# A decoder block on one core: other feed-forward groups, a mixer that ends earlier, and operands that are split where they land

## The chip, the cores and the metric

The kernel runs on one core of one Trainium2 chip. The metric is the device time of one execution in microseconds (us). TensorE (PE) multiplies matrices, VectorE (DVE) and ScalarE (ACT) do elementwise work, GpSimd (POOL) and SyncE (SP) issue the transfers. Every engine works through its instructions in order, and an instruction that waits holds up those behind it on the same engine.

## The reference

One layer of a decoder, 2048 positions of width 1024, all in fp32:

```python
mod = (silu(c) @ w_ada + b_ada)                       # shift, scale, gate, twice
h = rms_norm(x, norm1_g) * (1 + sc1) + sh1
gq, gk, gv, gr, glr, aq, ak, av = split(h @ w_in)
y_gla = gla_group(gq, gk, gv, log_sigmoid(glr @ w_gate + b) / 16, gr, gla_norm_g)   # 4 heads
y_att = dilated_attention_group(rms_norm(aq), rms_norm(ak), av)                     # 8 heads, 3 dilations
x = x + g1 * (concat(y_gla, y_att) @ w_out)
h = rms_norm(x, norm2_g) * (1 + sc2) + sh2
u_gate, u_val = split(causal_depthwise_conv(h @ w_up, conv_w, conv_b))              # width 3
x = x + g2 * ((silu(u_gate) * u_val) @ w_down)
```

w_up has 2 x 2816 columns, that is 22 pairs of 128-column blocks (a gate half and a value half); w_down has 2816 rows, 22 tiles of 128. The gated linear attention normalises its output per head by 1 / sqrt(mean square + eps).

## The kernel before

The sequence is cut into four chunks of 512 positions; everything is kept transposed, channels on the 128 partitions and positions along the row. An fp32 operand is split into a high part (rounded for the fast matmul) and a low part (the rest), and `mm3` (L308) makes each product of three matmuls: high by high, high by low, low by high. Weights are loaded as raw blocks of 512 KB on POOL's queue (L243), cast by ScalarE into whi (L248) and subtracted by VectorE into wlo (L249); `plan` (L258) lists the blocks in the order of their use and `weights` (L297) runs three blocks ahead, over two raw and four high and low slots.

The work is written as generators, and each `yield` ends a step. `beside(a, na, b, nb)` runs the steps of b and after each of them na/nb steps of a; what is left of a comes at the end. In `run` (L1159) the projections of all four chunks form `gemm` (27 of its steps are taken first). Then mixer 0 runs beside the rest of `gemm`, mixer 1 beside output projection 0 and feed-forward 0, mixer 2 beside output projection 1 and feed-forward 1, mixer 3 beside the next pair, and the last pair alone. The last steps of `gemm` are the channel blocks q6, g2, q7 and g3 of chunk 3's projection. A scheduler that simulates the program takes this order as its priorities and fixes the order of the instructions on each engine when the program is built; slots of a tile pool are waited for when none is free.

A mixer (`mix`, L1054) has two halves of gated linear attention (`gla`, L668) and four pairs of dilated attention heads (`attn`, L825). Each half ends with the per-head norm (L796 to L802): Ln and Exp on ScalarE make the inverse root. Each pair of heads ends with an addition into a stage tile (L1050) that is stored as block 4 + hp of y in DRAM (L1051).

`outproj` (L1062) loads the eight blocks of y (L1067) into tiles called sq, of which there are three, and splits each into hhi (ScalarE, L1076) and hlo (VectorE, L1077). For chunk 0 most of these parts lie in the slots ghi and glo (five each), which the q blocks of the projection use too; for the other chunks they lie in hhi and hlo (ten each), eight of which hold the feed-forward operand of the chunk before until its last up product. `soon` (L353) ties each load to a matmul some 20 contraction steps back. Eight blocks of 24 matmuls follow, evicted with the residual by VectorE (L1083), then the second norm's statistics, then the put-off product `self.tail`, and then the normalised and modulated operand (L476, L478, L480).

`ffn` (L1091) goes over groups of gate tiles: four, four, four, four, four and two. For each group it makes the up products (L1104, two blocks of 24 matmuls a tile), the conv (L1106 to L1113), the gate and its split into ghi and glo (L1117 to L1123), and then the down product of the group before (`down`, L1133): eight output blocks of three matmuls a gate tile, each added to the residual on VectorE (L1151). The last group's down product is not made there: it becomes `self.tail` and runs in the next chunk's output projection, after its eight blocks. Because the residual's tiles serve the next chunk by then, the next-to-last down product stores its eight blocks to DRAM (L1155), and the put-off one loads them again (L1148) into the slots y0 and y1 (two each), adds, and stores the result (L1153). Chunk 0's output projection has the last gate block of chunk 3's projection (`wide(1)`) as its tail. Four PSUM banks (psg) serve all of these products, four others (psa) the mixers.

Of the kernel before, what the change touches and what calls it, by code (L numbers as in the profile page):

```python
# [2 lines left out]

# [1 line left out]

# [5 lines left out]
F32 = mybir.dt.float32  # L11
# [8 lines left out]
P = 128  # L20
T = 512
NCH = 4
KD = 8
NF = 22
EPS = 1e-6
BIG = 1e30
GATE = 6
FIRST = (0, 1, 2, 3)
LEAD = 1

# [109 lines left out]
def chain(*gs):  # L140
    for g in gs:
        yield from g


class K:
# [112 lines left out]
    def plan(self):  # L258

        def proj(c):  # L260
            for o in ORDER if c else ORDER0:
                b = int(o[1])
                if c == NCH - 1 and o == "W1":
                    continue
                if o[0] == "W":
                    yield from (("w_tokw", (b, j), 2, T) for j in range(4))
                elif o[0] == "V":
                    yield from ((f"w_av{b}", (j,), 4, 256 if b else 272) for j in range(2))
                else:
                    b += 4 * (o[0] == "q")  # L270
                    if c or b not in FIRST:
                        yield "w_ch", (b,), KD, P

        def down(g):
            n = min(4, NF - 4 * g)
            yield from (("w_down", (4 * g + q,), n, 1024 // n) for q in range(n))

        def ffn(c):
            for g in range(6):
                for f in range(4 * g, min(4 * g + 4, NF)):  # L280
                    yield from (("w_up", (f + NF * half,), KD, P) for half in range(2))
                if g:
                    yield from down(g - 1)
            if c == NCH - 1:
                yield from down(5)

        for c in range(NCH):
            yield from proj(c)
        for c in range(NCH):
            yield from (("w_out", (b,), KD, P) for b in range(KD))  # L290
            if c:
                yield from down(5)
            else:
                yield from (("w_tokw", (1, j), 2, T) for j in range(4))
            yield from ffn(c)
# [372 lines left out]
    def gla(self, c, a):  # L668
# [106 lines left out]
        for s in range(2):  # L775
# [17 lines left out]
                nc.scalar.activation(jk[:, hd * P:(hd + 1) * P], o[:, hd * P:(hd + 1) * P], AF.Square, accum_out=ss[:, s, hd:hd + 1])  # L793
            os.append(o)
            yield
        nc.scalar.activation(ss, ss, AF.Ln, bias=self.eps, scale=1.0 / P)  # L796
        nc.scalar.activation(ss, ss, AF.Exp, scale=-0.5)
        ys = []
        for s in range(2):
            y = t2("pt", 5)  # L800
# [24 lines left out]
    def attn(self, c, hp, ready):  # L825
# [222 lines left out]
        st = self.at.tile([P, T], F32, name="stage", bufs=2)  # L1048
        nc.scalar.copy(st.rearrange("p (l j r) -> p r j l", j=4, r=4), O16.rearrange("p (r j l) -> p r j l", r=4, j=4))
        nc.vector.tensor_tensor(st.rearrange("p (l r) -> p r l", r=16), O.rearrange("p (r l) -> p r l", r=16), st.rearrange("p (l r) -> p r l", r=16), op=ALU.add)  # L1050
        nc.sync.dma_start(D[c]["y"][4 + hp], st)  # L1051
        yield

    def mix(self, c):  # L1054
# [7 lines left out]
    def outproj(self, c):  # L1062
        nc, A = self.nc, self.A
        hs = []
        for k in range(KD):
            t = self.tmp.tile([P, T], F32, name="sq", bufs=3)
            ld = self.dq.dma_start(t, self.D[c]["y"][k])  # L1067
            self.soon(ld)

            if c or k > 5:  # L1070
                hi, lo = (self.hp.tile([P, T], F32R, name=n) for n in ("hhi", "hlo"))
            elif k == 5:
                hi, lo = (self.up.tile([P, T], F32R, name=n, tag=n) for n in ("y0", "y1"))
            else:
                hi, lo = (self.gp.tile([P, T], F32R, name=n, tag=n) for n in ("ghi", "glo"))
            nc.scalar.copy(hi, t)  # L1076
            nc.vector.tensor_tensor(lo, t, hi.bitcast(F32), op=ALU.subtract)  # L1077
            hs.append((hi, lo))
        x1 = self.load_x(c)
        for cb in range(KD):  # L1080
            ps = self.pg()
            self.mm3(ps, self.weights("w_out", cb), hs)
            nc.vector.scalar_tensor_tensor(x1[cb], ps, self.mod[:, 16 + cb:17 + cb], x1[cb], op0=ALU.mult, op1=ALU.add)  # L1083
            yield
        self.x1[c] = x1
        rstd = self.norm_stats(lambda k: x1[k], not c)
        yield from self.tail
        self.h2[c] = self.norm_mod(lambda k: x1[k], rstd, self.G2, self.mod[:, 24:32], True)


    def ffn(self, c):  # L1091
        nc, A = self.nc, self.A
        x1, h2 = self.x1[c], self.h2[c]
        groups = [list(range(i, min(i + 4, NF))) for i in range(0, NF, 4)]
        pend = None
        for gi, grp in enumerate(groups + [None]):
            gs = []
            if grp is not None:
                for f in grp:
                    ys = []  # L1100
                    for half in range(2):
                        b = f + NF * half
                        ps = self.pg()
                        self.mm3(ps, self.weights("w_up", b), h2)  # L1104
                        y = self.up.tile([P, T], F32, name=f"y{half}")
                        nc.scalar.activation(y, ps, AF.Identity, bias=self.cb[:, b:b + 1], scale=self.cw[:, 2, b:b + 1])  # L1106
                        nc.vector.scalar_tensor_tensor(y[:, 1:], ps[:, :T - 1], self.cw[:, 1, b:b + 1], y[:, 1:], op0=ALU.mult, op1=ALU.add)  # L1107
                        nc.vector.scalar_tensor_tensor(y[:, 2:], ps[:, :T - 2], self.cw[:, 0, b:b + 1], y[:, 2:], op0=ALU.mult, op1=ALU.add)  # L1108
                        if c > 0:
                            nc.vector.scalar_tensor_tensor(y[:, :1], self.halo[:, b, 1:2], self.cw[:, 1, b:b + 1], y[:, :1], op0=ALU.mult, op1=ALU.add)  # L1110
                            nc.vector.scalar_tensor_tensor(y[:, :2], self.halo[:, b], self.cw[:, 0, b:b + 1], y[:, :2], op0=ALU.mult, op1=ALU.add)
                        if c < NCH - 1:
                            nc.scalar.copy(self.halo[:, b], ps[:, T - 2:])  # L1113
                        ys.append(y)
                        yield
                    th = self.up.tile([P, T], F32, name="th", bufs=1)
                    nc.scalar.activation(th, ys[0], AF.Tanh, scale=0.5)  # L1117
                    nc.vector.scalar_tensor_tensor(th, th, 1.0, ys[0], op0=ALU.add, op1=ALU.mult)
                    nc.vector.scalar_tensor_tensor(ys[1], th, 0.5, ys[1], op0=ALU.mult, op1=ALU.mult)
                    ghi = self.gp.tile([P, T], F32R, name="ghi", tag="ghi")  # L1120
                    nc.scalar.copy(ghi, ys[1])
                    glo = self.gp.tile([P, T], F32R, name="glo", tag="glo")
                    nc.vector.tensor_tensor(glo, ys[1], ghi.bitcast(F32), op=ALU.subtract)  # L1123
                    gs.append((ghi, glo))
            if pend is not None:
                d = self.down(c, *pend)
                if grp is None and c < NCH - 1:
                    self.tail = d
                else:
                    yield from d  # L1130
            pend = (gi, gs)

    def down(self, c, gj, pgs):  # L1133


        nc, A = self.nc, self.A
        n = len(pgs)
        cols = 1024 // n
        defer = c < NCH - 1
        for q in range(1024 // cols):  # L1140
            w = self.weights("w_down", gj * 4 + q)
            for cc in range(cols // P):
                cb = (q * cols) // P + cc
                ps = self.pg()
                self.mm3(ps, [(wh[:, cc * P:(cc + 1) * P], wl[:, cc * P:(cc + 1) * P]) for wh, wl in w], pgs)
                if gj == 5 and defer:
                    x1 = self.up.tile([P, T], F32, name="x1", tag=f"y{cb % 2}")
                    self.dq.dma_start(x1, self.D[c]["x1"][cb])  # L1148
                else:
                    x1 = self.x1[c][cb]  # L1150
                nc.vector.scalar_tensor_tensor(x1, ps, self.mod[:, 40 + cb:41 + cb], x1, op0=ALU.mult, op1=ALU.add)  # L1151
                if gj == 5:
                    self.dq.dma_start(A["outT"][c, cb], x1)  # L1153
                elif gj == 4 and defer:
                    self.dq.dma_start(self.D[c]["x1"][cb], x1)  # L1155
                yield


    def run(self):  # L1159
# [101 lines left out]
        gemm = along(self.ada_late(), 66, chain(ahead(1), ahead(2), ahead(3), proj(3)), 94)  # L1261
        for _ in range(27):
            next(gemm)
        beside(self.mix(0), 68, gemm, 72)
        beside(self.mix(1), 68, chain(self.outproj(0), self.ffn(0)), 90)
        beside(self.mix(2), 68, chain(self.outproj(1), self.ffn(1)), 86)
        beside(self.mix(3), 68, chain(self.outproj(2), self.ffn(2)), 90)
        for _ in chain(self.outproj(3), self.ffn(3)):
# [9 lines left out]

def pack_down(w):
    out = []  # L1280
    for g in range(6):
        n = 4 if g < 5 else 2
        out.append(pack_blocks(w[g * 512:g * 512 + n * P], 1024 // n))
    return np.concatenate(out)


# [44 lines left out]
```

## Time and profile before

| | |
|---|---|
| median of 3 runs | 2582.25 us (2578.29 to 2584.26) |
| profiled execution | 2578.59 us |
| its span, first to last instruction | 2576.8 us |
| TensorE busy | 2543.0 us, 99% |
| VectorE, ScalarE, GpSimd busy | 74%, 49%, 17% |
| mean granted TensorE clock | 0.999 |
| HBM | 157 GB/s over the span |

The profiled execution is one run of the program; its own time stands 3.7 us under the median. In the rows of a window stand, for each engine, the busy time and the number of instructions that started in it, then the granted TensorE clock, the share of the 16 DMA engines, and GB/s. In the rows in order of time stand start, duration, engine, line, operation, output and inputs, number, and in brackets the idle time before, with what ended it. In the rows of groups stand the busy time, the mean of one in ns and the idle time before. A wait row names who waited for whom, the total, how often, and the longest.

### The profile page before, as it was taken

What the parts mean: (1) busy time and instruction counts of PE and PEld (TensorE: products, weight loads), DVE (VectorE), ACT (ScalarE), POOL (GpSimd) and SP (SyncE); (2) the same over time, 40 slices, a digit from 0 to 9 for tenths busy, and PEclk for the clock granted to TensorE, in tenths of its full rate; (3) what the DMA queues carried; (4) which work ended last, traced back from release to release, by engine and by line L of the source; (5) the groups of instructions that cost most, each with busy time, mean ns of one, the idle gap of its engine ahead of it and who ended that gap; (6) DMA issues with size and microseconds to landing.
All of it is one profiled execution on the core that took longest, in us unless ns stands there. A gap on an engine that the chain in (4) does not pass through costs nothing.

```text
span 2576.8 us, 49715 instructions
## 1 busy us (share of the span) xinstructions
PE 2543.0 (99%) x19458; PEld 2096.0 (81%) x19458; DVE 1899.6 (74%) x4111; ACT 1264.6 (49%) x2624; POOL 449.2 (17%) x818
## 2 busy tenths in 40 slices
PE   7999999999999999999999999999999999999999
PEld 4888888888788888887888888878888888788887
DVE  7678877867688766677977777689777775766665
ACT  5556655656454444454545444346444443433332
POOL 2333432323210000022100000310000003200001
PEclk9999999999999999999999999999999999999999
DMA  8876665756633444456334444743444535433232
GB/s 326 266 242 203 223 226 178 239 169 211 211 111 99 128 133 128 134 178 203 123 108 130 141 139 117 248 141 112 127 137 136 146 106 198 150 98 98 98 99 82
DMA packets 190622, 408.47 MB, mean 159 GB/s; under 512 B 48642, under 2 KB 89652, under 8 KB 189108
## 3 DMA queue, kind: packets, MB, share of 16 engines
q0 software_dynamic: 88416, 309.64, 37.0%
q1 hardware_dynamic: 101972, 95.65, 12.7%
q8 instruction: 154, 2.52, 0.4%
q14 instruction: 80, 0.66, 0.1%
HBM read 342.30 MB, written 62.91 MB: 157 GB/s over the span
## 4 chain that ended last, share of the span: by engine, by line
PE 94%; DVE 2%; issue 1%; DMA 1%; ACT 1%; POOL 1%; SPq 0%; POOLq 0%; DVEq 0%; ACTq 0%
PE psg L314 27%; PE psg L315 27%; PE psg L316 27%; PE psa L1028 2%; PE psa L902 2%; PE psa L876 2%; PE psa L709 2%; PE psa L1023 1%; PE psa L925 1%; PE psa L782 1%; PE psa L781 1%; PE psa L456 0%; PE psa L786 0%; PE psg L1200 0%; PE psa L1047 0%
## 5 line engine op out<-in xcount | busy, mean ns | idle before, releaser
L314 PE MATMUL psg<-hhi,whi 128*128 128x512 f32 x1968 | 771.2, 394 | 4.8 <-DVE x L1151 3.3
L315 PE MATMUL psg<-hlo,whi 128*128 128x512 f32 x1968 | 769.7, 392 | 2.2 <-DVE hlo L1077 1.9
L316 PE MATMUL psg<-hhi,wlo 128*128 128x512 f32 x1968 | 769.3, 392 | 0.7 <-DVE wlo L249 0.7
L248 ACT CAST whi<-wraw 128x1024 fp32r<-128x1024 f32 (+1 forms) x388 | 407.1, 1051 | 472.4 <-PE psg L315 360.7
L249 DVE TENSOR_TENSOR wlo<-wraw,whi 128x1024 fp32r<-128x1024 f32 (+1 forms) x388 | 474.5, 1223 | 202.7 <-ACT whi L248 194.4
L314 PEld LDWEIGHTS psg<-hhi,whi 128*128 128x128 f32 x1968 | 369.4, 188 | 84.9 <-ACT hhi L478 5.9
L316 PEld LDWEIGHTS psg<-hhi,wlo 128*128 128x128 f32 x1968 | 369.5, 188 | 78.6 <-DVE wlo L249 1.1
L315 PEld LDWEIGHTS psg<-hlo,whi 128*128 128x128 f32 x1968 | 369.6, 188 | 78.4 <-DVE hlo L1077 2.3
L314 PE MATMUL psg<-ghi,whi 128*128 128x512 f32 x744 | 294.6, 398 | 0.1
L315 PE MATMUL psg<-glo,whi 128*128 128x512 f32 x744 | 292.0, 393 | 0.4 <-DVE glo L1077 0.4
L316 PE MATMUL psg<-ghi,wlo 128*128 128x512 f32 x744 | 291.1, 391 | 0.7 <-DVE wlo L249 0.7
L243 POOL DMA_DIRECT2D wraw<-in_w_up_dram x176 | 96.4, 548 | 979.2 <-DVE wlo L249 814.8
L1151 DVE SCALAR_TENSOR_TENSOR x<-psg,mod,x 128x512 f32<-128x512 f32 x192 | 143.1, 748 | 112.4 <-PE psg L316 111.5
L314 PE MATMUL psg<-whi,hhi 128*128 128x512 f32 (+2 forms) x512 | 172.8, 342 | 2.9 <-ACT stg L582 1.4
L315 PE MATMUL psg<-wlo,hhi 128*128 128x512 f32 (+2 forms) x512 | 173.2, 339 | 0.0
L316 PE MATMUL psg<-whi,hlo 128*128 128x512 f32 (+2 forms) x512 | 173.0, 341 | 0.0
L314 PEld LDWEIGHTS psg<-ghi,whi 128*128 128x128 f32 x744 | 140.0, 188 | 31.3 <-issue 1.4
L316 PEld LDWEIGHTS psg<-ghi,wlo 128*128 128x128 f32 x744 | 139.9, 188 | 30.0 <-DVE wlo L249 1.1
L315 PEld LDWEIGHTS psg<-glo,whi 128*128 128x128 f32 x744 | 140.0, 188 | 28.9 <-DVE glo L1077 0.8
L1106 ACT ACTIVATE y<-psg,tables_sb 128x512 f32<-128x512 f32 x176 | 136.0, 775 | 3.0 <-PE psg L316 2.0
L1107 DVE SCALAR_TENSOR_TENSOR y<-psg,tables_sb,y 128x511 f32<-128x511 f32 x176 | 130.8, 744 | 2.8 <-ACT y L1106 2.7
L1108 DVE SCALAR_TENSOR_TENSOR y<-psg,tables_sb,y 128x510 f32<-128x510 f32 x176 | 130.8, 743 | 0.8
(271 smaller groups left out, 3604.0 us busy)
## 6 DMA issues: line engine op xcount, KB each, us to landing
wraw<-in_w_up_dram POOLq DMA_DIRECT2D x176, 512.0 KB, 3.8
wraw<-in_w_down_dram POOLq DMA_DIRECT2D x88, 512.0 KB, 3.8
wraw<-in_w_ch_dram POOLq DMA_DIRECT2D x44, 512.0 KB, 4.6
wada<-in_w_ada_dram POOLq DMA_DIRECT2D x64, 256.0 KB, 5.1
wraw<-in_w_tokw_dram POOLq DMA_DIRECT2D x32, 512.0 KB, 5.0
wraw<-in_w_out_dram POOLq DMA_DIRECT2D x32, 512.0 KB, 4.2
sq<-in_xT_dram POOLq DMA_DIRECT2D x48, 256.0 KB, 4.5
x<-x POOLq DMA_DIRECT2D x48, 256.0 KB, 5.6
```

Of the source, the lines that this page charges most:

```text
L243: ld = self.dq.dma_start(raw[:, :n], src)
L248: nc.scalar.copy(hi[:, :n], raw[:, :n])
L249: nc.vector.tensor_tensor(lo[:, :n], raw[:, :n], hi[:, :n].bitcast(F32), op=ALU.subtract)
L314: nc.tensor.matmul(ps, wh, hh, start=first and k == 0, stop=False, skip_group_check=shared)
L315: nc.tensor.matmul(ps, wh, hl, start=False, stop=False, skip_group_check=shared)
L316: self.lastmm = nc.tensor.matmul(ps, wl, hh, start=False, stop=k == n - 1, skip_group_check=shared)
L709: nc.tensor.matmul(sp[j:j + w, o + n * w:o + (n + 1) * w], kh[R, k0:k0 + w], qh[R, q0:q0 + w], start=True, stop=True)
L876: nc.tensor.matmul(at(i, hh, o, n)[H[z]], q(H[hh], i, z), key(H[hh], i, k0, n), start=True, stop=True, skip_group_check=True)
L1106: nc.scalar.activation(y, ps, AF.Identity, bias=self.cb[:, b:b + 1], scale=self.cw[:, 2, b:b + 1])
L1107: nc.vector.scalar_tensor_tensor(y[:, 1:], ps[:, :T - 1], self.cw[:, 1, b:b + 1], y[:, 1:], op0=ALU.mult, op1=ALU.add)
L1108: nc.vector.scalar_tensor_tensor(y[:, 2:], ps[:, :T - 2], self.cw[:, 0, b:b + 1], y[:, 2:], op0=ALU.mult, op1=ALU.add)
L1151: nc.vector.scalar_tensor_tensor(x1, ps, self.mod[:, 40 + cb:41 + cb], x1, op0=ALU.mult, op1=ALU.add)
```

## The change

The groups of feed-forward tiles become 4, 4, 4, 4, 2, 4, so that the next-to-last down product has two tiles and the last, put-off one has four; `plan` and the host's packing of w_down follow. Mixer 0 runs beside the first 68 of the remaining projection steps, and the rest of `gemm` stands ahead of output projection 0 beside mixer 1. In the output projection the y blocks are loaded into the slot of the low part itself, ScalarE makes the high part of it and VectorE subtracts in place; the eighth block is not stored and loaded but taken from the mixer's stage tile. In the per-head norm, Sqrt on ScalarE and a reciprocal on VectorE take the place of Ln and Exp.

```diff
+GROUPS = (4, 4, 4, 4, 2, 4)
+STARTS = (0, 4, 8, 12, 16, 18)
...
         def down(g):
-            n = min(4, NF - 4 * g)
-            yield from (("w_down", (4 * g + q,), n, 1024 // n) for q in range(n))
+            n = GROUPS[g]
+            yield from (("w_down", (STARTS[g] + q,), n, 1024 // n) for q in range(n))
 
         def ffn(c):
             for g in range(6):
-                for f in range(4 * g, min(4 * g + 4, NF)):
+                for f in range(STARTS[g], STARTS[g] + GROUPS[g]):
...
-        nc.scalar.activation(ss, ss, AF.Ln, bias=self.eps, scale=1.0 / P)
-        nc.scalar.activation(ss, ss, AF.Exp, scale=-0.5)
+        nc.scalar.activation(ss, ss, AF.Sqrt, bias=self.eps, scale=1.0 / P)
+        nc.vector.reciprocal(ss, ss)
...
-        nc.sync.dma_start(D[c]["y"][4 + hp], st)
+        if hp < 3:
+            nc.sync.dma_start(D[c]["y"][4 + hp], st)
+        else:
+            self.ylast = st
         yield
...
         for k in range(KD):
-            t = self.tmp.tile([P, T], F32, name="sq", bufs=3)
-            ld = self.dq.dma_start(t, self.D[c]["y"][k])
-            self.soon(ld)
-
             if c or k > 5:
                 hi, lo = (self.hp.tile([P, T], F32R, name=n) for n in ("hhi", "hlo"))
             elif k == 5:
                 hi, lo = (self.up.tile([P, T], F32R, name=n, tag=n) for n in ("y0", "y1"))
             else:
                 hi, lo = (self.gp.tile([P, T], F32R, name=n, tag=n) for n in ("ghi", "glo"))
+            t = self.ylast if k == KD - 1 else lo.bitcast(F32)
+            if k < KD - 1:
+                self.soon(self.dq.dma_start(t, self.D[c]["y"][k]))
             nc.scalar.copy(hi, t)
             nc.vector.tensor_tensor(lo, t, hi.bitcast(F32), op=ALU.subtract)
...
-        groups = [list(range(i, min(i + 4, NF))) for i in range(0, NF, 4)]
+        groups = [list(range(i, i + n)) for i, n in zip(STARTS, GROUPS)]
...
-            w = self.weights("w_down", gj * 4 + q)
+            w = self.weights("w_down", STARTS[gj] + q)
...
-        beside(self.mix(0), 68, gemm, 72)
-        beside(self.mix(1), 68, chain(self.outproj(0), self.ffn(0)), 90)
+        beside(self.mix(0), 68, islice(gemm, 68), 68)
+        beside(self.mix(1), 68, chain(gemm, self.outproj(0), self.ffn(0)), 94)
```

More of the change, by code (lines that the diff above doesn't have):

```diff
@@ L2 @@
 from contextlib import ExitStack
+from itertools import islice
 import numpy as np
@@ L1280, in pack_down @@
     out = []
-    for g in range(6):
-        n = 4 if g < 5 else 2
-        out.append(pack_blocks(w[g * 512:g * 512 + n * P], 1024 // n))
+    for i, n in zip(STARTS, GROUPS):
+        out.append(pack_blocks(w[i * P:(i + n) * P], 1024 // n))
     return np.concatenate(out)
```

## The prediction

> **What bounds the kernel now.** I read the page first (busy shares and the chain that ended last), then the waits of TensorE alone, then single places in order of time.
>
> ```profile
> span 2576.8 us, 49715 instructions
> PE 2543.0 (99%) x19458; PEld 2096.0 (81%) x19458; DVE 1899.6 (74%) x4111; ACT 1264.6 (49%) x2624; POOL 449.2 (17%) x818
> PE 94%; DVE 2%; issue 1%; DMA 1%; ACT 1%; POOL 1%; SPq 0%; POOLq 0%; DVEq 0%; ACTq 0%
> ...
> PE psa L456 <- ACT sq L1193: 14.1, 1, 14.1
> PE psg L314 <- DVE x L1151: 3.3, 2, 1.7
> PE psg L315 <- DVE hlo L1077: 1.9, 1, 1.9
> PE psg L314 <- ACT hhi L478: 1.5, 1, 1.5
> PE psg L316 <- DVE wlo L249: 1.4, 2, 0.7
> ```
>
> TensorE is the bound: 94% of the chain, and idle for 2576.8 - 2543.0 = 33.8 us, of which 14.1 us are the start, which the change doesn't touch. A busy TensorE is not one at its peak, so the unit price comes from a stretch with nothing but feed-forward products, and the end from the last one:
>
> ```profile
> 2400.00:2500.00 100.00, 100.00 (x443) 82.81 (x442) 63.93 (x103) 35.31 (x43) 10.09 (x19) 1.00 0.30 95
> 2500.00:2577.00 77.00, 71.97 (x318) 59.27 (x316) 43.94 (x63) 18.30 (x22) 8.60 (x16) 1.00 0.26 89
> ```
>
> 100 / 443 = 0.226 us for one 128x512 product. A down block over four gate tiles is 12 of them, 2.71 us, over two tiles 1.35 us; eight blocks make 21.7 or 10.8 us. The 5.0 idle us at the end (last eviction and store) stay: the last block is evicted and stored as before. So 33.8 - 14.1 - 5.0 = 14.7 us of idle time is all that a better order can win, save for what slow restarts and a slow clock hide in busy time. The change adds and removes no large product.
>
> **The longer put-off product.** Today the put-off down product has two gate tiles (48 products, 10.8 us). It is followed by the first up products of the next chunk, and there TensorE stops in chunk 1, and alike in 2 and 3 (TensorE, VectorE and GpSimd in order of time):
>
> ```profile
> 1220.00 0.39 PE L316 MATMUL psg<-ghi,wlo 128*128 128x512 f32 x1
> 1222.03 0.47 PE L314 MATMUL psg<-hhi,whi 128*128 128x512 f32 x1 [1.64 <-DVE x L1151]
> 1222.60 0.50 PE L315 MATMUL psg<-hlo,whi 128*128 128x512 f32 x1
> ...
> 1719.49 0.47 PE L314 MATMUL psg<-hhi,whi 128*128 128x512 f32 x1 [1.65 <-DVE x L1151]
> ...
> 2212.14 0.47 PE L314 MATMUL psg<-hhi,whi 128*128 128x512 f32 x1 [1.47 <-ACT hhi L478]
> ...
> 1211.47 0.75 DVE L1151 SCALAR_TENSOR_TENSOR x<-psg,mod,x 128x512 f32<-128x512 f32 x1
> 1212.73 2.06 DVE L1151 SCALAR_TENSOR_TENSOR x<-psg,mod,x 128x512 f32<-128x512 f32 x3
> 1221.14 0.75 DVE L1151 SCALAR_TENSOR_TENSOR x<-psg,mod,x 128x512 f32<-128x512 f32 x1
> ...
> 1212.51 0.55 POOL L1153 DMA_DIRECT2D out_dram<-x  x1
> 1217.29 1.22 POOL L1148 DMA_DIRECT2D x<-x  x2 [1.66 <-DMA out_dram<-x]
> ```
>
> The residual of the put-off product goes through four SBUF slots (y0 and y1, two each): block 4 can be evicted only when block 0 was stored (1212.51) and the slot reloaded (issued 1217.29), at 1221.14. From block 0's eviction (1211.47) that is a round trip of 9.7 us. Blocks 4 to 7 lie finished in the four PSUM banks meanwhile, and the first up product has none. In the third place the normalised operand is last instead (L478). With four tiles a block comes every 2.71 us, so block 4 is finished 4 x 2.71 = 10.8 us after block 0, behind the 9.7 us round trip, and the norm has 10.8 us more. Both waits lose their ground. Each place costs its idle time (1.64 + 1.65 + 1.47 = 4.8 us) and slow restarts: starts 0.57 us apart at 1222.03 against 0.226, and more than the idle time alone from 1220.00 to 1222.03 (2.03 - 0.23 = 1.80). Upper end about 2.2 us a place, 6.6 us; lower end 0, if the wait goes elsewhere. I take 6.0, near the rows, as the cover doubles.
>
> The same groups **halve another cover**. The product between the last up block and the next output projection was four tiles (21.7 us) and is now two (10.8 us). In it lie the eight residual evictions and stores (one per 1.35 us now), the last gate tile's conv chain, weight splits, and the loads and splits of the projection's operands. In chunk 2's end:
>
> ```profile
> 2132.00:2153.90 21.90, 21.90 (x99) 18.12 (x98) 15.38 (x21) 7.45 (x11) 12.30 (x23) 1.00 0.77 266
> ...
> 2147.42 2.11 DVE L1077 TENSOR_TENSOR hlo<-sq,hhi 128x512 fp32r<-128x512 f32 x3 [0.74 <-ACT hhi L1076]
> 2156.13 1.89 DVE L1077 TENSOR_TENSOR hlo<-sq,hhi 128x512 fp32r<-128x512 f32 x3
> 2164.07 1.37 DVE L1077 TENSOR_TENSOR hlo<-sq,hhi 128x512 fp32r<-128x512 f32 x2 [6.05 <-ACT hhi L1076]
> ...
> sq<-y POOLq DMA_DIRECT2D x32, 256.0 KB, 6.3
> x<-in_xT_dram POOLq DMA_DIRECT2D x32, 256.0 KB, 6.2
> ```
>
> VectorE was busy 15.4 of these 21.9 us. If all of it had to be done in 10.8 us, it would be late by 4.6 us. But the operands needn't all be there: the product began at about 2154 with three of eight split, took the others as they came, and no TensorE wait of that kind stands in its list but the 0.7 us on a weight split. With four PSUM banks open, one operand pair feeds 4 x 3 x 0.226 = 2.7 us. Bounds for three places: nothing, or 3 x 4.6 = 13.8 us; a gain of 0.7 if that weight split comes sooner. I take 0.7 a place, the one wait seen inside such a product: 2.1 us. In the last chunk the final product has four tiles and its last gate tile only 10.8 us of cover, and TensorE can go on over three tiles in four banks for 4 x 9 x 0.226 = 8.1 us more: nothing.
>
> **Operands split in place.** Each y block is loaded into the slot of its own low part, no longer through three sq slots. In the rows above the three slots show: splits in threes, the last two 8 us after. Now the loads can leave together once the slots are free, seven issues of 0.55 us (as L1153's above) on POOL's queue. The first now waits there for an hlo slot; behind it stand the residual's stores, input loads and weight loads, and ScalarE's weight casts wait for the last of these: 3.9 us, within the weights' run-ahead of three blocks (24 x 0.226 = 5.4 us each). First operand: 0.55 + 6.3 + a cast and a subtraction of 0.7 each (2.11 for three) = 8.3 us after the last up product, inside 10.8; with no cover it would be 8.3 us a place. I count what may show within the 0.7. The eighth operand stays in SBUF: four stores on SP's queue and four loads on POOL's fall away.
>
> **First mixers four steps early.** The output projection of chunk 0 waited for its last operands:
>
> ```profile
> 673.62 1.19 PE L314 MATMUL psg<-hhi,whi 128*128 128x512 f32 x4
> 676.71 0.50 PE L315 MATMUL psg<-hlo,whi 128*128 128x512 f32 x1 [1.89 <-DVE hlo L1077]
> ...
> 647.00:651.00 4.00, 2.65 (x47) 1.95 (x45) 2.51 (x3) 3.16 (x6) 0.39 (x1) 1.00 1.00 327
> 651.00:655.00 4.00, 3.68 (x40) 2.85 (x41) 4.00 (x8) 1.67 (x4) 1.07 (x3) 0.57 1.07 315
> 400.00:600.00 200.00, 200.00 (x1731) 170.34 (x1731) 149.94 (x425) 122.00 (x291) 62.77 (x111) 1.00 0.65 207
> ```
>
> Now mixer 0 is written out beside 68 steps, and q6, g2, q7, g3 follow: 4 x 24 x 0.226 = 21.7 us between the mixer's end and the projection, with the eighth block in SBUF. The 1.89 us and the restart (0.45) can go: bounds 2.3 us won, or a second such wait on the tiles that q7 shares, 1.9 lost; I take 2.0 won. The granted clock was 0.57 for 4 us where the mixer's small matmuls stood alone: 4 x 0.43 = 1.7 us. With projection steps among them it need not come again; between 0 and 1.7 I take half, 0.9. The price: mixer 0 advances 1.00 steps a projection step, not 0.94, VectorE's load there going from 75% (149.9 of 200) to at most 80%, hidden by its idle fifth; without that cover 6% of the mixer's VectorE work would show, some us.
>
> [...]
>
> **Ln and Exp to Sqrt and a reciprocal**, eight calls:
>
> ```profile
> L796 ACT ACT_TABLE_LOAD x7 | 9.0, 1283 | 0.1
> L797 ACT ACT_TABLE_LOAD x7 | 9.0, 1283 | 0.1
> L797 ACT ACTIVATE gss<-gss 128x8 f32<-128x8 f32 x8 | 1.7, 208 | 0.1
> L982 DVE RECIPROCAL M<-M 128x8 f32<-128x8 f32 x16 | 3.2, 203 | 0.5
> ```
>
> Fourteen table loads go, and at most sixteen come (Sqrt, and the next Exp or Tanh): up to 2.6 us more on an engine at 49%, while the chain to the normalised output loses a load (1.28 us). The reciprocal costs VectorE 8 x 0.2 = 1.6 us, the Exp's 1.7 go from ScalarE. All of it lies beside TensorE; I take 0.4 us of loss for this and the faster mixer, between 0 and 2.6.
>
> **The sum.** -6.0 + 2.1 - 2.0 - 0.9 + 0.4 = -6.4 us. The profiled execution took 2578.6 us (span 2576.8 and 1.8 around it), which becomes 2572.2. The median shown is 2582.25, 3.7 us above it; on that base it is 2575.8, my forecast.
>
> **Rivals.**
> 1. *The halved cover is paid in full (slower).* At the starts of output projections 1 to 3 VectorE is late by 4.6 us each: 13.8 instead of 2.1, so +5.3 us, 2587.5. It decides from 8.5 / 3 = 2.8 us a place. For it: VectorE's 15.4 us and 266 GB/s at a 0.77 share, both to be pressed into half the time. Against it: the products that begin with three operands, and the in-place loads.
> 2. *The put-off product doesn't do what it says.* The first up product waits for the norm's operands (as in the third place) or for evictions that the order puts late; a third of the 6.0 comes: -2.4 us, 2579.9. For it: the order on each engine is fixed when the program is built, and L478's wait; against: 10.8 us more for both.
> 3. *Nothing is paid back:* 6.6 + 2.3 + 1.7 + 0.7 = 11.3 us, 2571.0. Every stall named would have to go and none come.
> 4. *Table switches on the path.* If Ln and Exp had mostly shared one table, eight loads would be added, 8 x 1.283 = 10.3 us of ScalarE, and evictions of up products behind them would hold PSUM banks: 2575.8 + 10.3 = 2586.1. The seven loads at each line speak against it. [...]
>
> **How the numbers follow.** Forecast (3.5 to 9.5 us won, 2572.8 to 2578.8) 0.50; rival 1 0.12, rival 2 0.20, rival 3 0.14, rival 4 0.04. The range 2568 to 2585 reaches past rival 3 by the runs' own spread (2578.3 to 2584.3, 3 us each way) and leaves out most of rivals 1 and 4. A measurement of this kernel tells about 0.2%, 5.2 us, from no change. Faster than 2577.1: three quarters of the forecast's chance and rival 3, 0.52. Slower than 2587.4: half of rival 1 and the tails, 0.12. The rest, 0.36, is the same.
>
> **What would show it.** After: no L1151 or L478 wait of TensorE at the first up products of chunks 1 to 3; no hlo wait at chunk 0's projection; granted clock 1.0 throughout; L1077 splits no longer in threes. I am wrong if TensorE waits for hlo, hhi or evictions at the starts of projections 1 to 3 by over 2.8 us each, or if its idle time stays at 33 us.

## The result and the profile after

The changed kernel takes 2575.82 us (median of 13 runs, 2573.89 to 2578.23), the kernel before 2582.25 (13 runs on the same chip, 2578.29 to 2587.31): a ratio of 0.9975, 95% interval 0.9968 to 0.9983, 6.4 us less. The profiled execution took 2574.43 us. The page of the changed kernel, and its list of TensorE's waits (who waited for whom, total, how often, longest):

```profile
span 2572.6 us, 49697 instructions
PE 2541.9 (99%) x19458; PEld 2099.0 (82%) x19458; DVE 1900.2 (74%) x4119; ACT 1271.4 (49%) x2624; POOL 445.6 (17%) x814
...
PE psa L459 <- ACT sq L1198: 14.2, 1, 14.2
PE psg L317 <- ACT ghi L1081: 3.5, 1, 3.5
PE psa L527 <- DVE sqr L521: 2.7, 1, 2.7
PE psa L928 <- DMA qf<-q: 2.5, 1, 2.5
```

Line numbers are 3 to 5 higher than before (mm3 is L317 to L319, the residual's eviction L1156, the splits L1081 and L1082). The waits for the residual (3.3 us), for the normalised operand hhi (1.5), and for hlo (1.9) are gone, that for wlo fell from 1.4 to 0.3, but three new ones of 2.5 to 3.5 us stand in their place, all ahead of the first feed-forward. Behind it TensorE is never idle: the stretch from there to the last product, and in it the place where chunk 1's first up product waited 1.64 us before (TensorE in order of time), the seven y loads of chunk 1 (GpSimd), and its splits (one line's instructions):

```profile
742.00:2567.00 1825.00, 1825.00 (x13803) 1510.44 (x13802) 1332.63 (x2896) 824.70 (x1744) 222.65 (x411) 1.00 0.43 133
...
1227.19 0.39 PE L319 MATMUL psg<-ghi,wlo 128*128 128x512 f32 x1
1227.42 0.39 PE L317 MATMUL psg<-hhi,whi 128*128 128x512 f32 x1
1227.64 0.39 PE L318 MATMUL psg<-hlo,whi 128*128 128x512 f32 x1
...
1138.33 3.72 POOL L1080 DMA_DIRECT2D hlo<-y  x7 [3.54 <-PE psg L319]
...
L1082 DVE TENSOR_TENSOR hlo<-hlo,hhi x7: 681/693/699, 1143.1 to 1154.6; 128x512 fp32r<-128x512 f32 x7
L1082 DVE TENSOR_TENSOR hlo<-stage,hhi x1: 700/700/700, 1155.2 to 1155.2; 128x512 fp32r<-128x512 f32 x1
```

The up products follow the put-off one at the full pace of 0.23 us; the loads go out in one bunch, and the eighth split reads the stage tile. Over the whole span TensorE's idle time fell only from 33.8 to 30.7 us (2572.6 - 2541.9), since output projection 0 is another picture (TensorE in order of time, then windows with PE, PEld, DVE, ACT and POOL busy, the granted clock, the DMA share, GB/s):

```profile
655.24 0.50 PE L527 MATMUL psa<-sqr,blk 128*128 128x512 f32 x1
659.26 1.65 PE L317 MATMUL psg<-ghi,whi 128*128 128x512 f32 x3 [3.52 <-ACT ghi L1081]
...
663.67 0.63 PE L318 MATMUL psg<-glo,whi 128*128 128x512 f32 x1
664.10 0.63 PE L319 MATMUL psg<-ghi,wlo 128*128 128x512 f32 x1
...
655.00:659.00 4.00, 0.74 (x23) 0.32 (x10) 4.00 (x8) 3.72 (x8) 2.66 (x5) 0.77 1.07 285
659.00:663.00 4.00, 3.64 (x69) 2.55 (x70) 4.00 (x8) 3.10 (x9) 2.90 (x6) 0.50 1.05 372
663.00:667.00 4.00, 4.00 (x11) 3.12 (x10) 3.96 (x10) 0.36 (x2) 1.20 (x3) 0.50 1.03 399
```

At clock 0.50 one 128x512 product starts 0.43 us after another instead of 0.23. Summed over the profile, the clock was halved for 17.1 us (near 298, 377 and 657 us), before for 3.4 (what lies behind the last product is left out).

**Where the time went.** I cut each profile at one instruction: the 2784th product of mm3, the last ahead of feed-forward 0. What lies before its start is the head; from there to the start of the last product of mm3 but one is the body.

```profile
728.37 0.39 PE L316 MATMUL psg<-whi,hlo 128*128 128x512 f32 x1
...
2571.35 0.39 PE L315 MATMUL psg<-glo,whi 128*128 128x512 f32 x1
```

These rows are of the kernel before (head 728.4, body 1843.0); in the changed one the two stand at 740.2 and 2567.4 (body 1827.2). So the body is 15.8 us shorter and the head 11.8 longer. Some of both is work that moved: with the early mixer 108 more small products, those of the mixers, are done in the head (2856 against 2748), worth 5.6 us (experiment 3).

### The profile page after: what moved, and what is told of

It is laid out like the page before. It is cut to its first block, busy times and chain, and to the rows that moved or that the text cites. A ratio compares the mean times of both kernels' runs of the same rounds, so it can differ in the third digit from the quotient of the medians.

```text
span 2572.6 us, 49697 instructions
## 1 busy us (share of the span) xinstructions
PE 2541.9 (99%) x19458; PEld 2099.0 (82%) x19458; DVE 1900.2 (74%) x4119; ACT 1271.4 (49%) x2624; POOL 445.6 (17%) x814
## 4 chain that ended last, share of the span: by engine, by line
PE 78%; DVE 1%; issue 1%; DMA 0%; POOL 0%; ACT 0%; POOLq 0%; ACTq 0%
PE psg L317 23%; PE psg L318 23%; PE psg L319 23%; PE psa L1031 2%; PE psa L905 2%; PE psa L879 2%; PE psa L712 1%; PE psa L1026 1%; PE psa L928 1%; PE psa L785 0%; PE psa L784 0%; PE psa L789 0%; PE psa L1050 0%; PE psa L811 0%; DMA glo<-y 0%
## 5 line engine op out<-in xcount | busy, mean ns | idle before, releaser
L317 PE MATMUL psg<-hhi,whi 128*128 128x512 f32 x1968 | 773.2, 394 | 0.0
L319 PE MATMUL psg<-hhi,wlo 128*128 128x512 f32 x1968 | 769.9, 391 | 0.0
L252 DVE TENSOR_TENSOR wlo<-wraw,whi 128x1024 fp32r<-128x1024 f32 (+1 forms) x388 | 475.0, 1224 | 205.3 <-ACT whi L251 198.7
L317 PEld LDWEIGHTS psg<-hhi,whi 128*128 128x128 f32 x1968 | 370.0, 188 | 77.8 <-issue 0.8
L319 PEld LDWEIGHTS psg<-hhi,wlo 128*128 128x128 f32 x1968 | 370.0, 188 | 76.8 <-issue 0.3
L317 PE MATMUL psg<-ghi,whi 128*128 128x512 f32 x744 | 296.7, 400 | 3.5 <-ACT ghi L1081 3.5
L319 PE MATMUL psg<-ghi,wlo 128*128 128x512 f32 x744 | 292.7, 393 | 0.0
L1156 DVE SCALAR_TENSOR_TENSOR x<-psg,mod,x 128x512 f32<-128x512 f32 x192 | 143.3, 749 | 125.7 <-PE psg L319 125.1
L317 PE MATMUL psg<-whi,hhi 128*128 128x512 f32 (+2 forms) x512 | 173.5, 344 | 1.3 <-ACT stg L585 0.7
L319 PE MATMUL psg<-whi,hlo 128*128 128x512 f32 (+2 forms) x512 | 173.4, 341 | 0.0
L317 PEld LDWEIGHTS psg<-ghi,whi 128*128 128x128 f32 x744 | 140.4, 189 | 34.1 <-ACT ghi L1081 3.8
L319 PEld LDWEIGHTS psg<-ghi,wlo 128*128 128x128 f32 x744 | 140.2, 188 | 29.5 <-issue 0.2
```

Of the source, the lines that this page charges most:

```text
L252: nc.vector.tensor_tensor(lo[:, :n], raw[:, :n], hi[:, :n].bitcast(F32), op=ALU.subtract)
L317: nc.tensor.matmul(ps, wh, hh, start=first and k == 0, stop=False, skip_group_check=shared)
L319: self.lastmm = nc.tensor.matmul(ps, wl, hh, start=False, stop=k == n - 1, skip_group_check=shared)
```

## The experiments

The whole set, with head and body from one profile each, ratios against the kernel before on the same chip, and the time at half clock (the stretch behind the last product left out). The kernels were measured in four groups, each beside the kernel before, whose median was 2582.25 us for the change, 2583.64 for the four single parts, 2582.63 for the change without Sqrt and the two rows under it, and 2585.39 for the change again and the last three rows; so across groups only the ratios compare. The one profile of a kernel can lie up to 4.5 us from its median:

| kernel | median us | ratio, 95% interval | head | body | half clock |
|---|---|---|---|---|---|
| before | 2582.25 | 1 | 728.4 | 1843.0 | 3.4 |
| before, again (1 run) | 2587.47 | | 737.5 | 1842.7 | 13.7 |
| change | 2575.82 | 0.9975 (0.9968 to 0.9983) | 740.2 | 1827.2 | 17.1 |
| change, again | 2577.80 | 0.9967 (0.9955 to 0.9979) | 745.6 | 1827.2 | 20.5 |
| groups alone | 2581.32 | 0.9989 (0.998 to 0.9999) | 730.3 | 1842.3 | 6.8 |
| early mixer alone | 2590.36 | 1.0023 (1.0014 to 1.0032) | 738.7 | 1843.0 | 13.7 |
| in-place part alone | 2579.41 | 0.9983 (0.9974 to 0.9993) | 729.4 | 1841.8 | 13.7 |
| Sqrt alone | 2585.49 | 1.0009 (0.9998 to 1.002) | 731.1 | 1843.4 | 6.8 |
| change without Sqrt | 2574.08 | 0.9965 (0.9952 to 0.9978) | 744.3 | 1827.1 | 20.5 |
| change without early mixer | 2573.02 | 0.9959 (0.9944 to 0.9975) | 737.2 | 1833.0 | 13.7 |
| groups and in-place part | 2571.12 | 0.9949 (0.9933 to 0.9966) | 732.5 | 1832.7 | 10.2 |
| change without in-place part | 2580.21 | 0.9981 (0.9969 to 0.9992) | 740.2 | 1831.6 | 13.7 |
| groups, eighth operand kept | 2573.36 | 0.9951 (0.9934 to 0.9968) | 729.9 | 1835.2 | 3.4 |
| groups, in-place loads | 2577.01 | 0.9965 (0.9952 to 0.9978) | 734.8 | 1837.9 | 17.1 |

**1. The four parts, each alone.** Each is the kernel before with one part of the diff (its main lines):

```diff
# groups
+GROUPS = (4, 4, 4, 4, 2, 4)
# early mixer
-        beside(self.mix(0), 68, gemm, 72)
+        beside(self.mix(0), 68, islice(gemm, 68), 68)
# in place
+            t = self.ylast if k == KD - 1 else lo.bitcast(F32)
# Sqrt
-        nc.scalar.activation(ss, ss, AF.Ln, bias=self.eps, scale=1.0 / P)
-        nc.scalar.activation(ss, ss, AF.Exp, scale=-0.5)
+        nc.scalar.activation(ss, ss, AF.Sqrt, bias=self.eps, scale=1.0 / P)
+        nc.vector.reciprocal(ss, ss)
```

> Only the feed-forward groups 4,4,4,4,2,4. Theory (the longer put-off product earns everything, the rest of the change loses): the three waits of TensorE at the first up products of chunks 1 to 3 are gone and nothing comes at the starts of output projections 1 to 3; 7 to 10 us faster than before (2572 to 2575), more than the whole change. Rival (the halved cover needs the in-place loads): waits for hhi or hlo appear at the starts of projections 2 and 3, and the gain is under 4 us.

> Only the first mixer beside 68 steps instead of 72. Theory (the denser mixer costs the 6 us by which the change is behind at the start of output projection 0): 3 to 7 us slower than before, with half-clock stretches or waits of TensorE for mixer data between 250 and 660 us. Rival (the Sqrt's table loads cost them): within 2 us of before or faster by up to 2, as the hlo wait at 676 us goes.

> Only the output projection's operands split in place and the eighth block kept in SBUF. Theory: the loads leave together, but TensorE hardly waited for them, so within 2 us of before. Rival (the in-place loads earn a part of the gain of chunks 1 to 3): 3 to 5 us faster.

> Only Sqrt and reciprocal instead of Ln and Exp in the per-head norm. It has 39 table loads instead of 30 (9 x 1.283 = 11.5 us of ScalarE). Theory (ScalarE has room): within 1.5 us of before. Rival (the loads hold up the q blocks of the projection, and through them TensorE): 3 to 6 us slower, all of it before 660 us.

Measured against the median of before beside them (2583.64): groups -2.3 us, early mixer +6.7, in place -4.2, Sqrt +1.9, together +2.1, where the change as a whole gives -6.4. The interval of the groups ends just under 1 and that of Sqrt holds 1, so these two are hardly told from nothing. The groups fell short of their theory (7 to 10 us), with the rival's size but at projection 1 and not at 2 and 3; the early mixer has its theory's size; the in-place part came out as its rival said; Sqrt lies between its two. So the parts act on each other. The groups alone show how. Their boundaries between chunks run without the waits, but output projection 1 loses what they gain (the groups alone: waits of TensorE; then GpSimd, ScalarE and TensorE in order of time):

```profile
PE psg L318 <- DVE wlo L251: 3.6, 3, 2.3
PE psg L316 <- ACT hhi L1078: 2.0, 1, 2.0
...
1170.47 0.55 POOL L1069 DMA_DIRECT2D sq<-y  x1 [10.29 <-issue]
...
1173.76 0.62 ACT L1078 CAST hhi<-sq 128x512 fp32r<-128x512 f32 x1 [7.42 <-DMA sq<-y]
1176.97 1.98 ACT L250 CAST whi<-wraw 128x1024 fp32r<-128x1024 f32 x2
...
1174.43 1.20 PE L316 MATMUL psg<-hhi,whi 128*128 128x512 f32 x4 [2.03 <-ACT hhi L1078]
1182.68 0.50 PE L318 MATMUL psg<-hhi,wlo 128*128 128x512 f32 x1 [2.26 <-DVE wlo L251]
1184.04 0.63 PE L316 MATMUL psg<-hhi,whi 128*128 128x512 f32 x1
```

The eighth operand's load goes out only at 1170.47, because its store, issued at 1153.81, took 15.5 us to land; GpSimd waited 10.3 us for that. ScalarE stands 7.42 us before the cast, and the weight casts come behind it (1176.97), so TensorE waits twice, for the operand and then for a weight, and goes on at half clock (a row of 0.63 us, 0.39 at full clock). In the kernel before, load and cast of this operand are about as late (1167.38 and 1174.45), but the projection begins at 1159.16 and here at 1150.71: the halved cover took that slack.

**2. Which half of the in-place part removes that loss.** The groups with only the eighth operand kept in SBUF, and with only the loads in place (the eighth still by way of DRAM):

```diff
# eighth operand kept
+            if k == KD - 1:
+                t = self.ylast
+            else:
+                t = self.tmp.tile([P, T], F32, name="sq", bufs=3)
# in-place loads
+            t = lo.bitcast(F32)
+            self.soon(self.dq.dma_start(t, self.D[c]["y"][k]))
```

> The groups 4,4,4,4,2,4 and, of the in-place part, only the eighth operand kept in SBUF: operands 1 to 7 still go through the three sq slots. Nothing else of the change. Theory (the eighth operand's late way through DRAM makes the loss of 6.8 us at output projection 1 in the groups alone, and the in-place loads don't): the waits on hhi (2.0 us) and wlo (3.6 us) near 1175 to 1183 us are gone, and the time is that of groups and in-place together, 0.994 to 0.996 of the kernel before (about 2570 to 2573 us). Rival (the three slots of sq make the loss, as seven loads still pass through them): the waits stay, and the ratio is that of the groups alone, 0.998 to 1.000.

> The groups 4,4,4,4,2,4 and, of the in-place part, only the loads: all eight operands are loaded into the slots of their low parts, the eighth too, which is still stored to DRAM and loaded again. Theory (the eighth operand's way through DRAM makes the loss): TensorE still waits 2 us or more for the eighth operand at output projection 1, and the ratio is that of the groups alone, 0.998 to 1.000. Rival (the three slots make the loss): no wait over 1 us there, ratio 0.994 to 0.996.

The windows at output projection 1, each to about the start of the put-off product: groups alone, then with the eighth kept (as many products), then in-place loads, then both parts (again as many as each other). The first two begin with the projection, the last two about 4 us ahead of it:

```profile
1150.50:1205.00 54.50, 49.97 (x425) 40.18 (x424) 35.38 (x55) 20.45 (x36) 10.20 (x19) 0.97 0.64 212
```

```profile
1150.00:1197.00 47.00, 47.00 (x424) 38.77 (x423) 33.97 (x54) 19.86 (x34) 10.36 (x20) 1.00 0.78 242
```

```profile
1151.00:1207.00 56.00, 54.05 (x509) 43.58 (x508) 38.48 (x61) 19.74 (x34) 12.15 (x23) 0.97 0.67 216
...
1176.05 0.62 ACT L1076 CAST hhi<-hlo 128x512 fp32r<-128x512 f32 x1 [3.98 <-DMA hlo<-y]
```

```profile
1149.00:1200.00 51.00, 51.00 (x507) 42.23 (x506) 37.70 (x61) 19.23 (x32) 11.34 (x22) 1.00 0.73 238
```

Counted from the projection's first product to the start of the put-off one, the stretch takes 54.5 us with the groups alone, 47.4 with the eighth kept, 52.1 with the in-place loads and 47.5 with both. So keeping the eighth operand removes the whole loss of 7.2 us, and with the in-place loads alone 4.6 us of loss stay: ScalarE still waits 3.98 us for that operand. The theory on the place holds, but not all its figures: with the loads alone TensorE waits only 0.4 us for that operand and 1.0 for a weight, not 2, with 3.4 us at half clock behind them, and the ratio lies between the theory's and the rival's. The loads shorten ScalarE's wait from 7.42 to 3.98 us. They gain elsewhere too: the body with both parts (1832.7) is 2.5 us shorter than with the eighth kept alone (1835.2), and that difference arises at output projection 3.

**3. The change with one part left out.** Each is the changed kernel with one part (in one case two) put back as it was before, again by main lines:

```diff
# without Sqrt
-        nc.vector.reciprocal(ss, ss)
+        nc.scalar.activation(ss, ss, AF.Exp, scale=-0.5)
# without early mixer; groups and in-place part: without both
-        beside(self.mix(0), 68, islice(gemm, 68), 68)
+        beside(self.mix(0), 68, gemm, 72)
# without in-place part
+            t = self.tmp.tile([P, T], F32, name="sq", bufs=3)
+            ld = self.dq.dma_start(t, self.D[c]["y"][k])
```

> The whole change, but with Ln and Exp kept in the per-head norm. By adding up the single parts (Sqrt alone cost 1.9 us): 2 us faster than the change, 8 us faster than before (about 2575). Rival (Sqrt's place in the order matters only beside the mixer's q blocks, where the change has table loads too): 4 us or more faster than the change.

> The whole change, but with mixer 0 beside all remaining projection steps as before. Theory (the four steps cost 6.7 us alone, and cost it in the change too): 13 us faster than before, 6 to 7 faster than the change, with no wait for the q tile and less half-clock time before 660 us. Rival (with the operands split in place the early end pays at output projection 0): the same as the change or up to 3 us slower.

> Only the groups and the in-place split. Theory (the two need each other: alone they gave 2.3 and 4.2 us, and the groups alone lost 7 us at output projection 1 to the eighth operand's late load): 11 to 16 us faster than before, the best version. Rival (their gains only add): 6.5 us, as the whole change.

> The change without its in-place part: groups, first mixer early, and Sqrt with a reciprocal; the operands go through the three sq slots and the eighth through DRAM, as before. Theory (the halved cover is free only with the in-place part): the loss of the groups alone comes back at output projection 1, TensorE waits there for hhi and wlo 2 us or more each, and the time is 5 to 9 us above the change's, 2580 to 2585 us, 0.999 to 1.001 of the kernel before. Rival (the change's earlier order of mixers 1 to 3 gives that operand enough time): no such wait, and within 3 us of the change's time, ratio 0.9965 to 0.9985.

The first three were measured together. Groups and in-place part: 2571.12, 11.5 us under the kernel before, within its theory's 11 to 16. With the early mixer added 2574.08 (+3.0), with Sqrt added 2573.02 (+1.9). By these, the change would be 11.5 - 4.9 = 6.6 us faster than before; it was 6.4, and 7.6 when measured again. The intervals of the three overlap, so +1.9 for Sqrt, here as alone, isn't clear of the runs' spread. The early mixer costs half of what it costs alone (+6.7), and leaving it out earned less than its theory's 6 to 7 us. It shortens the body by 5.6 us (1832.7 to 1827.1), which is the moved work, since TensorE is never idle in either body. Alone it doesn't: its body stays at 1843.0 where 1837.4 would be due, one half-clock stretch of 3.4 us at 2220 us among the loss, and its head less the moved work, 733.1, lies between the two heads of before. So its loss alone is in the body, and is not fully explained. Groups and in-place part together beat both kernels; their waits hold none of the output projections 1 to 3:

```profile
span 2570.7 us, 49705 instructions
...
PE psa L458 <- ACT sq L1197: 14.4, 1, 14.4
PE psa L693 <- ACT lh L687: 2.6, 1, 2.6
PE psg L317 <- DVE y L1081: 1.7, 1, 1.7
```

(The 1.7 us is chunk 0's projection, at 678 us.) Without the in-place part the rival came nearer than the theory: 2580.21 against 2577.80 for the change measured beside it, +2.4. No hhi wait of 2 us comes back: the stretch at output projection 1 is 46.5 us there, 46.4 in the change. The waits are smaller and spread, two of about 1 us in the two-tile products ahead of projections 1 and 3; the first is for a residual eviction, as rival 1 of the prediction had it, but 1.3 us and not 4.6:

```profile
PE psg L317 <- DVE x L1154: 1.3, 1, 1.3
...
PE psg L317 <- ACT halo L1116: 1.0, 1, 1.0
```

So the loss of 7.2 us belongs to the groups with the mixers' old timing. With the early mixer the eighth operand is ready sooner (its store goes out 5.5 us before the projection's first product and lands in 6.8 us; in the groups alone it goes out 3.1 us behind it and lands in 15.5), and the in-place part is worth 2.4 us.

**4. Both kernels once more,** unaltered.

> The kernel before, unchanged, for a second profile. Theory (runs of one kernel differ by how many half-clock stretches of 3.4 us TensorE falls into, and the profile of before had one, with a time 3.7 us under its median): another count of stretches, in other places, and a span longer by about 1.7 us for each further one. Rival (the stretches belong to the program): one stretch, again at about 651 us.

> The changed kernel once more, unaltered, to see which of its differences stand in a second execution. Theory (the body behind the first up product of chunk 0 runs the same in every execution, the part before it doesn't): from the first to the last up eviction the time is that of the first profile within 1 us, while half-clock stretches before 700 us differ from the 17.1 us of the first, and with them the span, by up to 9 us. Rival (the early first mixer itself makes these stretches): again 14 us or more at half clock between 290 and 660 us, and the qf wait of 2.5 us again. Median 2573 to 2579 us, ratio 0.9965 to 0.9985 by both.

Each body came out the same within 0.3 us (1843.0 and 1842.7; 1827.2 twice), while the heads differ by 9.1 and 5.4 us. In the kernel before, three more stretches at 1.7 us each, the theory's price, make 5.1 of the 9.1 us; TensorE also stands idle 4.9 us longer in that head (28.1 against 23.2). The kernel before, again, had half-clock windows that its first profile doesn't show:

```profile
196.00:200.00 4.00, 4.00 (x27) 3.69 (x27) 3.78 (x10) 3.62 (x9) 3.39 (x7) 0.57 0.83 278
656.00:660.00 4.00, 3.29 (x73) 2.51 (x73) 4.00 (x7) 2.19 (x6) 0.94 (x2) 0.62 1.05 343
660.00:664.00 4.00, 4.00 (x11) 3.13 (x10) 4.00 (x7) 1.71 (x5) 2.67 (x6) 0.52 1.05 350
684.00:688.00 4.00, 3.72 (x9) 3.02 (x10) 0.83 (x2) 0.00 (x0) 0.00 (x0) 0.57 0.00 0
```

For the changed kernel the rival's signs stand too, though kernels without the early mixer have up to 17.1 us at half clock as well, so the sum alone doesn't show that the mixer makes it. Of its 20.5 us 17.1 begin between 300 and 663 us, with the same waits for ghi, sqr and qf (the changed kernel again):

```profile
PE psg L317 <- ACT ghi L1081: 3.5, 1, 3.5
...
PE psa L527 <- DVE sqr L521: 2.7, 1, 2.7
PE psa L928 <- DMA qf<-q: 1.9, 1, 1.9
```

The wait for qf stands in all five profiles with the early mixer (1.9 to 4.5 us), each time with half-clock time between 375 and 387 us, and in none of the others' lists of TensorE's waits. The queue of SyncE and TensorE show where it is from, in the changed kernel and then in the kernel before:

```profile
366.06 1.99 SPq L814 DMA_DIRECT2D y<-stage  x2
374.13 1.59 SPq L825 DMA_DIRECT2D qf<-q  x2
...
376.90 0.89 PE L928 MATMUL psa<-kt,qf 64*32 64x32 f32 x64 [2.47 <-DMA qf<-q]
378.12 0.43 PE L318 MATMUL psg<-wlo,hhi 128*128 128x272 f32 x1
```

```profile
367.51 1.23 SPq L811 DMA_DIRECT2D y<-stage  x2
371.20 1.08 SPq L822 DMA_DIRECT2D qf<-q  x2
...
385.46 0.88 PE L925 MATMUL psa<-kt,qf 64*32 64x32 f32 x64
```

qf takes its slot from the two of stage, which the store of the linear attention's output still holds; SyncE waits for that store in both kernels. Before, the load went out at 371.20 for a product at 385.46, 14.3 us ahead. In the changed kernel the product stands 8.6 us earlier, at 376.90, but the load 2.9 us later, at 374.13: the store, though issued earlier, took up to 8.9 us to land instead of 3.7. A third slot for stage would test this; it wasn't tried.

## Why the prediction was right or wrong

The time was right (2575.8 forecast, 2575.82 measured), and so was the sign; but of the five terms one was right, and the errors of the others nearly cancel, so the close agreement is luck. Of the signs that the prediction names, the waits on L1151, L478 and hlo are gone and the splits no longer come in threes; the clock, though, wasn't 1.0 throughout.

- **Longer put-off product, -6.0:** held. Between the kernel before and groups with the in-place part, compared where equally many large and small products are done, the three chunk starts gain about 2.6, 2.3 and 2.1 us, 7.0 together, just over my upper bound of 6.6. The waits on L1151 and L478 at these places are gone in every kernel with the groups, so rival 2 is out.
- **Halved cover, +2.1:** mis-sized, and on a wrong ground. It costs nothing in the change. I looked at VectorE's load and at the operands in threes; the price that exists is the eighth operand's late way through DRAM and ScalarE's queue behind it: 7.2 us at one place in the groups alone, none with that operand kept. I had written that step into the in-place part only as four stores and four loads less. Rival 1 (4.6 us at each of three places) didn't come, though one place without the cover of the in-place part cost more than that.
- **In-place part:** I counted it within the 0.7 us a place; alone it gives -4.2 us by the medians, of which the bodies show 1.2 (1843.0 to 1841.8), although a half-clock stretch of 3.4 us, worth 1.7, fell into its body at 1224 us. The two heads are 728.4 and 729.4, so the profiles don't show where the rest lies.
- **First mixers early, -2.0, and the half-clock stretch, -0.9:** wrong in sign. The hlo wait of 1.89 us did go, but a ghi wait of 3.5 us came at the same projection (its first load went out at 651.25, right behind a weight load that had waited 3.18 us on GpSimd's queue, and landed at 658.44), and qf's 2.5 earlier. The ghi wait stands in the three profiles with the early mixer and the in-place part; the sum's bound for such a wait was 1.9. Costed by the medians, the step is +3.0 us in the change. The step that failed is "with projection steps among them it need not come again": half clock went from 3.4 to 17.1 us, 10.2 of it at this projection. Not all of that is the mixer's, since kernels without it have 3.4 to 17.1 us; what all five profiles with it show and no other is the wait for qf. I had priced the faster mixer only by VectorE's load, not by what its first attention heads wait for.
- **Sqrt and table loads, +0.4 with the faster mixer (0 to 2.6):** Sqrt alone is +1.9, within the range, but not for the reason given. "Fourteen table loads go, and at most sixteen come" was wrong: the profile before has 30 table loads, the changed one 38. The fourteen at Ln and Exp became eight at Sqrt, and fourteen new ones stand at other lines, such as four at the gate's tanh, which had none:

```profile
L799 ACT ACT_TABLE_LOAD x8 | 10.3, 1283 | 0.1
...
L1122 ACT ACT_TABLE_LOAD x4 | 5.1, 1283 | 0.1
```

  Rival 4 had this count, eight more, 10.3 us of ScalarE, but not their price: ScalarE is busy 49%, and 1.9 us show. One place where they show is the q blocks of the projection, near 300 us. All five profiles with Sqrt have waits for the squares there (sqr) of 2.4 to 3.7 us in all, the other nine at most 1.2; in Sqrt alone four table loads stand on ScalarE between 286.8 and 295.6 us, in the kernel before none (Sqrt alone):

```profile
PE psa L523 <- ACT sqr L517: 1.2, 1, 1.2
PE psa L524 <- DVE sqr L518: 1.2, 1, 1.2
```

  A half-clock stretch of 3.4 us follows in each of the five, and in one of the other nine. So the sqr wait of the changed kernel goes with Sqrt and not with the early mixer alone, and the rival of that experiment had the place right. Sqrt alone has 39 table loads. I had given eight more a chance of only 0.04, because Ln and Exp each showed seven.
- **Nothing paid back (rival 3, 2571.0):** not the change. The kernel without its early mixer and Sqrt, 2571.12, has that time, but not by that sum, in which the early mixer was to earn 4.0 us.

With the terms as measured: -7.0 at the chunk starts, -3.3 for the rest of the body (1843.0 - 1832.7 = 10.3 in all), +3.0 and +1.9 make -5.4 us, against -6.4 measured; the 1.0 us between lies within what the heads vary.

## What to carry to other kernels

When a cover is shortened, look for the operand that arrives last and for what is queued on the same engine behind its wait: here one operand's way through DRAM cost 7.2 us, since TensorE waited for it, then for a weight whose cast stood behind it, and went on at half clock, and keeping that one tile on chip removed the loss. When a stage is made faster, go through the loads that it needs first and the slots that they wait for; a load that goes out no sooner for an earlier use is a new stall (here qf's, 1.9 to 4.5 us). Cut profiles at a counted instruction before comparing them, since one part of the span may repeat within 0.3 us while another varies by 9.

## What the runs showed of the hardware

The granted clock isn't a property of the kernel alone: the same program had 3.4 us at half clock in one profile and 13.7 in another, all in the first 690 us, and the heads differ by 9.1 us. In all profiles the stretches ahead of the last product last 3.4, 6.8 or 10.2 us, by the mean clock of windows of 4 us (one of 3.4 us leaves 0.57). The one that begins at about 1183.3 us in the groups alone stands behind 2.26 us of idle time up to 1182.68. The length of the stall doesn't decide by itself: before, TensorE was busy 2.26 of the 4 us from 1220 on, with the wait of 1.64 us up to 1222.03, and the clock was 1.00 in the next 4 us; in the in-place part alone it was busy 2.25 of the same 4 us, and the clock was 0.57 in the next 4. What decides isn't shown. So one wait can cost its idle time in one run and 1.7 us more in another.
